# Layer one's last eight modulation groups: ScalarE multiplies and GpSimd adds, and TensorE sums over partitions only

## The chip, the cores and the metric

The kernel runs as one launch on one core of a Trainium2 chip. The core has five engines that the trace names PE (TensorE matrix multiplications; PEld is its weight load), DVE (VectorE), ACT (ScalarE), POOL (GpSimd) and SP (SyncE, which here only issues DMAs), and 16 DMA engines. Each engine works through its own list of instructions in order and waits for the others by semaphores. The metric is the device time of one execution in microseconds, lower is better.

## The reference, cut to what matters

The reference is a two-layer decoder trunk on 1,024 tokens of width 1,024. Per layer a mixer (a gated MLP, a dilated attention with 8 heads, and an S5 state-space part, on slices of one input projection `w_in`, joined by `w_out`) is followed by a grouped mixture of experts. Both are framed by layer norms that are shifted, scaled and gated by a modulation vector, and that vector is what the change is about:

```python
cond = silu(c)                                  # 1,024 numbers
for l in range(DEPTH):                          # two layers
    mod = cond @ ada_w[l] + ada_b[l]            # (1024) x (1024 x 6144): 25 MB of weights a layer
    sh1, sc1, g1, sh2, sc2, g2 = split(mod, 6)  # 1,024 columns each
    h = layer_norm(x) * (1 + sc1) + sh1
    ...                                         # mixer on h -> mix
    x = layer_norm(ALPHA * x + (1 + g1) * mix) * ln1_g[l] + ln1_b[l]
    h2 = layer_norm(x) * (1 + sc2) + sh2
    ...                                         # experts on h2 -> ffn
    x = layer_norm(ALPHA * x + (1 + g2) * ffn) * ln2_g[l] + ln2_b[l]
```

All of it is in float32.

## The kernel before, in words

**Modulation columns.** The 6,144 columns of a layer are worked in 12 groups of 512. A group is eight tiles `ada_w` of 128 partitions x 512 columns (256 KB), since the 1,024 rows lie as 8 rows on each of 128 partitions. Groups 0 to 3 of the first layer (sh1, sc1) are needed before anything else and have a function of their own, `ada_first`. The other eight (groups 4 and 5 are g1, 6 and 7 sh2, 8 and 9 sc2, 10 and 11 g2) are made by `ada` (L924), beside the main work. `ada` starts a second task that loads the eight tiles of each group in order into three buffers of the tag `ada_w`, and then has two forms, chosen by its last argument `pe`:

```python
if pe:                                           # before, for these eight groups
    yield ("until", self.fl.on(w)[1] + late)
    ...
    self.ada_mm(pb, self.csel[:, k], w, k == 0, k == 7)
    self.free(w)
    continue
yield ("until", self.fl.on(w)[1] + 0.5)
t = self.a.activation(w, w, AF.Copy, scale=self.csel[:, k, 0:1])   # ScalarE, in place
if acc is None:
    acc = w
else:
    yield ("until", t)
    self.g.tensor_add(acc, acc, w)                                 # GpSimd
    self.free(w)
...
self.ada_mm(pb, self.ones[:, 0:32], acc, True, True)               # once a group
```

`ada_mm` (L974) is four matrix multiplications of 128 columns, one for each quarter of the tile, on four quarters of the array. So the first form issues 8 x 4 of them a group, the second 4. In the trace each of these float32 multiplications leaves two records: four of them are a row "x8". In both forms `ada_end` (L979) adds the bias on DVE (`ada_m`) and stores the group in the DRAM row `modrow`; `ada_ready` then lets the readers go: the scaling of `w_out` by g1, the rows `sc` and `sh` ahead of the second norm, and the gate of the experts. The second layer's twelve groups already take the second form (calls at L2461 and L2528), six during the first layer's experts and six at the second layer's entry.

**Order of the work.** The kernel is written as tasks (Python generators) with priorities. While it is built, a planner (`Flow`, L115) steps through the tasks by a model of when each engine and each tile comes free, and the order in which instructions are recorded is the order in which every engine executes them. On the chip nothing is reordered. A change of one task's instructions therefore moves the others too.

**The first layer's stages.** Tokens are worked in eight tiles of 128. `project` multiplies each normalised tile (`hT`, split into two fp32r parts, three multiplications a product) with the columns of `w_in`: values and the S5 input, then the gated MLP's `uv`, then keys, then queries; these are the rows `bankA<-wu,hT`. Beside it the task `prep` makes the S5 weights of layer one (`ssm_setup`, `ssm_quarter`: tiles `s_CA`, `s_W`, `s_K`, `s_V`, with DVE and POOL working on them) and stores them as `ssm`. `s_turn` transposes the S5 input (`bankB<-ident,U`), `s5` runs the scan in four quarters (tiles `z`, `t1`, `X`; POOL clears a column of `X`), with the queries' weights let go when its second quarter loads. Attention (`kT`, `qT`, `PT`, `O`) follows, then the output projection (`mix`), then the experts.

Of the kernel before, what the change touches and what calls it, by code (L numbers as in the profile page):

```python
# [327 lines left out]
class Trunk:  # L328
# [2094 lines left out]
    def begin(self, l):  # L2423

        fl, I = self.fl, self.I
        ev = lambda n=NT: [Event() for _ in range(n)]
        self.a_ready, self.b_ready, self.q_ready, self.k_ready = ev(), ev(), ev(), ev()
        self.hT_ready, self.s_ready, self.mix_done, self.chosen = ev(), ev(), ev(), ev(2)
        self.c_ready, self.b_left, self.left, self.late_left = Event(), [4] * NT, [4, 4], 2 * NT
        self.pa_open, self.kq_open, self.at_open, self.s5_go = ev(4)  # L2430
        self.vc, self.vc_ready, self.entered = [None] * 2, ev(2), ev()
        self.hT, self.q = [None] * NT, [None] * NT
        pa_s, kq_s = ExitStack(), ExitStack()
        b = SimpleNamespace(pa_s=pa_s, kq_s=kq_s, prep=None, sb=None)
        if l:
            self.small = NT
            self.front(l)
        ln, bc = self.ln, self.bc
        if l == 0:
            st, sb = ExitStack(), ExitStack()  # L2440
            sets = self.ssm_loads(0, self.pool(sb, "ssm_in", "right"))
            tp = self.pool(st, "prm", "right")
            loads = self.param_loads(tp)
        if l:
            ins = [fl.spawn(self.enter_on(l, i, ln, bc), (0.5 if i < HANDED else 4.4) + i / 100) for i in range(NT)]
        else:
            ins = [fl.spawn(self.enter(l, t, ln, bc), t[0]-2) for t in ((0,), (1,), (2, 3), (4, 5), (6, 7))]
        uv, us, ua = self.w_first
        uk, uq = self.w_in(l, 1024), self.w_in(l, 512)
        if l == 0:  # L2450
            fl.spawn(self.ada_first(), -1)
            for u in uq:
                u.hold = self.s5_go
            for u in uv:
                u.more, u.hold = self.wpools, self.shifted
            self.weights([u for us in self.w_first for u in us] + uk + uq)

            fl.spawn(self.ada([(0, n) for n in range(4, 12)], self.hT_ready[1]), 4)
            b.sb, b.prep = sb, fl.spawn(self.prep(st, tp, loads, sets), 4)
        else:  # L2460
            fl.spawn(self.ada([(1, n) for n in range(6, 12)], self.hT_ready[3], 3.0, False), 4)  # L2461
            for u in uk:
                u.hold = self.s5_go
            self.weights(uk + uq)
        tails, gm, qk, vs = [], [], [], []
        task = lambda to, f, *a: to.append(fl.spawn(f(*a), 3))


        def first():
            yield from self.project([(uv, 512, lambda i, pb: task(vs, self.v_after, l, i, pb)),  # L2470
                                     (us, 256, lambda i, pb: task(tails, self.s_after, l, i, pb, ln))])


        def second():
            yield ("wait", m1)
            yield from self.project([(ua, 512, lambda i, pb: task(gm, self.gmlp, l, i, pb))])

        def keys():
            yield ("wait", m2)
            yield from self.project([(uk, 512, lambda i, pb: task(qk, self.k_after, i, pb))])  # L2480

        def queries():
            yield ("wait", mk)
            yield from self.project([(uq, 512, lambda i, pb: task(qk, self.q_after, i, pb))], True)
        m1 = fl.spawn(first(), 6 if l else 5)
        m2 = fl.spawn(second(), 5)
        mk = fl.spawn(keys(), 5)
        mq = fl.spawn(queries(), 5)

        def left():  # L2490
            yield ("wait", m2)
            for e in gm:
                yield ("wait", e)
            pa_s.close()
            self.pq = self.pool(kq_s, "pq", "left")
            self.kT = self.loose(self.pool(kq_s, "kT", "left").tile([128, 4, T], F32, name="kT"))
            self.kq_open.at = fl.now
        b.ins, b.m1, b.mq, b.left, b.tails, b.qk, b.vs = ins, m1, mq, left, tails, qk, vs
        return b
# [208 lines left out]
```

## Time and profile before

| what | us |
|---|---|
| runs (three) | 2178.49, 2185.55, 6393.65; median 2185.55 |
| the profiled execution, its own time | 2174.52 |
| its span, first to last instruction | 2172.7 |
| PE busy | 1939.7 (89%) |
| DVE busy | 1186.0 (55%) |
| ACT busy | 747.2 (34%) |
| POOL busy | 312.0 (14%) |
| `ada_w` groups on ACT (second form, 12 groups) | 67.3 |
| `ada_w` sums on POOL (second form, 12 groups) | 118.8 |

The profiled execution took 2174.52 us, 1.8 us more than its span; the two runs near it took 4 and 11 us longer. Busy shares are means over the whole span; the change lies between 57 and about 560 us of it. A row of groups reads: line, engine, operation, result <- operands, shapes, count | busy us, mean ns of one | idle us of the engine ahead of them and what ended most of it.

### The profile page before, as it was taken

How to read it: one execution, taken by the hardware profiler on the slowest of the kernel's cores; microseconds unless marked ns; L12 is line 12 of the kernel's file. 1: busy time of each engine (PE TensorE's matmuls, PEld its weight loads, DVE VectorE, ACT ScalarE, POOL GpSimd, SP SyncE). 2: the span in 40 equal slices, each digit the busy share in tenths (PEclk: the TensorE clock that was granted, in tenths of full speed). 3: DMA queues.
4: the chain of work that ended last, by engine and by line, in shares of the span. 5: the costliest groups of instructions: out<-in, count | busy, mean ns of one | idle time of the engine just before them, and what ended most of it. 6: DMA issues, size and time to landing. Idle time of an engine off the chain costs nothing. (4 is left out here: it accounts for less than half of the span.)

```text
span 2172.7 us, 32497 instructions
## 1 busy us (share of the span) xinstructions
PE 1939.7 (89%) x12034; PEld 1341.7 (62%) x12034; DVE 1186.0 (55%) x2891; ACT 747.2 (34%) x1372; POOL 312.0 (14%) x304
## 2 busy tenths in 40 slices
PE   5988999989899999897888989999799999999782
PEld 3866777668653656556557777766685465655640
DVE  7857634556862744435377575455576332443536
ACT  2321145533322424324247334564213131332431
POOL 0024000100113233210002211020000101111000
PEclk9999999999999999998889999999899999999896
DMA  7565632145748899897764544331673769989782
GB/s 267 176 200 167 228 131 79 51 150 179 270 160 293 254 332 341 292 320 234 265 184 161 175 121 126 94 104 59 209 239 126 260 217 309 318 309 306 214 294 100
DMA packets 186822, 451.51 MB, mean 208 GB/s; under 512 B 28968, under 2 KB 80376, under 8 KB 169636
## 3 DMA queue, kind: packets, MB, share of 16 engines
q1 hardware_dynamic: 169584, 393.60, 51.9%
q0 software_dynamic: 15584, 55.24, 10.5%
q8 instruction: 96, 1.57, 0.3%
q10 hardware_dynamic: 1492, 0.56, 0.1%
q14 instruction: 66, 0.54, 0.1%
HBM read 366.66 MB, written 83.01 MB: 207 GB/s over the span
## 5 line engine op out<-in xcount | busy, mean ns | idle before, releaser
L467 PE MATMUL bankA<-wu,hT 128*128 128x512 f32 (+2 forms) x3202 | 834.1, 415 | 27.4 <-DMA hT<-mixT 15.3
L467 PEld LDWEIGHTS bankA<-wu,hT 128*128 128x128 f32 (+1 forms) x3202 | 561.5, 190 | 208.8 <-issue 76.4
L467 PE MATMUL bankA<-hT 128*128 128x512 f32 (+1 forms) x834 | 260.2, 476 | 10.3 <-ACT hT L110 6.7
L110 DVE TENSOR_TENSOR wu<-raw,wu 128x1024 fp32r<-128x1024 f32 x122 | 151.7, 1248 | 161.7 <-ACT wu L110 160.6
L110 ACT ACTIVATE hT<-bankB 128x512 fp32r<-128x512 f32 (+1 forms) x174 | 99.4, 595 | 355.8 <-PE bankB L480 335.7
L467 PE MATMUL bankY<-wu,hT 128*128 128x512 f32 (+1 forms) x584 | 207.1, 520 | 5.0 <-ACT hT L110 4.1
L467 PEld LDWEIGHTS bankA<-hT 128*128 128x128 f32 (+1 forms) x834 | 143.4, 183 | 81.8 <-issue 43.5
L110 ACT ACTIVATE wu<-raw 128x1024 fp32r<-128x1024 f32 x122 | 128.8, 1060 | 157.3 <-DMA raw<-in_exp_w_gate_dram 40.6
L110 POOL TENSOR_TENSOR ada_w<-ada_w 128x512 f32<-128x512 f32 x84 | 118.8, 1415 | 349.8 <-ACT ada_w L110 343.5
L467 PEld LDWEIGHTS bankY<-wu,hT 128*128 128x128 f32 (+1 forms) x584 | 104.0, 188 | 76.3 <-issue 54.9
L110 DVE TENSOR_TENSOR hT<-bankB,hT 128x512 fp32r<-128x512 f32 x114 | 75.4, 686 | 113.8 <-ACT hT L110 113.7
L366 POOL DMA_INDIRECT xa<-g,rc_idx x40 | 68.4, 1709 | 460.2 <-DVE g L110 358.6
L110 DVE TENSOR_TENSOR hT<-raw,hT 128x1024 fp32r<-128x1024 f32 x61 | 75.9, 1249 | 86.0 <-ACT hT L110 85.6
L467 PE MATMUL bankY<-hT 128*128 128x512 f32 (+1 forms) x310 | 104.1, 511 | 8.7 <-ACT hT L110 8.4
L110 DVE SCALAR_TENSOR_TENSOR g<-bankY,rc_wsl,mod 128x512 f32<-128x512 f32 x68 | 48.4, 747 | 81.6 <-PE bankY L467 80.3
L467 PE MATMUL bankC<-wu,hT 128*128 128x512 f32 (+1 forms) x256 | 84.1, 480 | 6.1 <-ACT wu L110 2.1
L110 ACT ACTIVATE hT<-raw 128x1024 fp32r<-128x1024 f32 x61 | 64.4, 1059 | 71.3 <-DMA raw<-in_exp_w_up_dram 24.8
L110 ACT ACTIVATE ada_w<-ada_w,csel 128x512 f32<-128x512 f32 x96 | 67.3, 719 | 60.0 <-DMA ada_w<-in_ada_w_dram 58.4
L467 PEld LDWEIGHTS bankY<-hT 128*128 128x128 f32 (+1 forms) x310 | 53.8, 189 | 46.1 <-issue 24.0
L110 ACT ACTIVATE hT<-hT,mx 128x256 f32<-128x256 f32 (+7 forms) x128 | 70.8, 558 | 2.6 <-DVE mx L110 2.5
L480 PE MATMUL bankB<-ident,hT 128*128 128x128 f32 x384 | 62.4, 289 | 6.5 <-ACT hT L110 2.9
L110 ACT ACTIVATE mhT<-bankB 128x512 f32<-128x512 f32 x32 | 19.2, 599 | 141.7 <-PE bankB L480 141.7
(496 smaller groups left out, 2614.9 us busy)
## 6 DMA issues: line engine op xcount, KB each, us to landing
ada_w<-in_ada_w_dram SPq DMA_DIRECT2D x160, 256.0 KB
raw<-in_exp_w_gate_dram SPq DMA_DIRECT2D x48, 512.0 KB
raw<-in_exp_w_up_dram SPq DMA_DIRECT2D x48, 512.0 KB
raw<-in_exp_w_down_dram SPq DMA_DIRECT2D x48, 512.0 KB
wu<-in_exp_w_down_dram SPq DMA_DIRECT2D x23, 1024.0 KB
hT<-in_exp_w_up_dram SPq DMA_DIRECT2D x20, 1024.0 KB
wu<-in_exp_w_up_dram SPq DMA_DIRECT2D x19, 1024.0 KB
wu<-in_exp_w_gate_dram SPq DMA_DIRECT2D x19, 1024.0 KB
```

The costliest lines, as they stand in the source:

```text
L110: f(*a, **k)
L366: self.nc.gpsimd.indirect_dma_start(out=rows, out_offset=bass.IndirectOffsetOnAxis(ap=ix, axis=0), in_=x, in_offset=None, compute_op=OP.add)
L467: self.nc.tensor.matmul(out, l, r, start=start, stop=stop, **kw)
L480: self.nc.tensor.transpose(out, x, self.ident[:k, :k] if perm is None else perm)
```

## The change

One call is changed: the eight groups 4 to 11 of layer one now take the second form of `ada` instead of the first. Loads, bias, store and the waiting readers stay as they are written.

```diff
-            fl.spawn(self.ada([(0, n) for n in range(4, 12)], self.hT_ready[1]), 4)
+            fl.spawn(self.ada([(0, n) for n in range(4, 12)], self.hT_ready[1], 3.0, False), 4)
```

It removes 256 multiplications of TensorE (512 records) that stood in 48 places of its list, and adds 32 (64 records) in 8 places, 64 multiplications of ScalarE and 56 additions of GpSimd. The DMAs are the same; the planner places them, and much else, anew.

TensorE, in the gated MLP's part of the projection (`uv`, `gt` are the MLP's tiles, `s_CA`, `s_W` the S5 weights). Before:

```order
L467 MATMUL bankA<-wu,hT 128x512 x6
L480 MATMUL bankB<-ident,gt 128x128 x2
L467 MATMUL bankC<-ada_w,csel 32x128 x4
L467 MATMUL bankA<-wu,hT 128x512 x6
L467 MATMUL bankC<-ada_w,csel 32x128 x4
L480 MATMUL bankB<-ident,s_W 128x128 x4
L467 MATMUL bankA<-wu,hT 128x512 x12
L467 MATMUL bankB<-uv,gm_wt 128x64 x4
L467 MATMUL bankC<-ada_w,csel 32x128 x4
```

and now:

```order
L467 MATMUL bankB<-uv,gm_wt 128x64 x4
L467 MATMUL bankA<-wu,hT 128x512 x12
L480 MATMUL bankB<-ident,gt 128x128 x2
L467 MATMUL bankA<-wu,hT 128x512 x6
L480 MATMUL bankB<-ident,s_W 128x128 x4
L467 MATMUL bankA<-wu,hT 128x512 x6
L467 MATMUL bankB<-uv,gm_wt 128x64 x4
```

The small bursts are gone from between the projection's rows. In the whole list 48 bursts (36 of x4, 8 of x8, 4 of x12) have become 8 of x4.

GpSimd, from the last of the S5 weights (`s_W`) through the S5 scan (`X`) to the attention's stores (`mixT`). Before:

```order
L110 TENSOR_TENSOR s_W<-s_W,s_t_2272 128x256
L110 MEMSET zero 128x1024
L110 MEMSET ada_b 128x128
L110 MEMSET X 128x2 x6
L110 MEMSET ada_b 128x128
L110 MEMSET X 128x2 x2
L356 DMA mixT_73<-hT 128x4x128 x16
```

and now:

```order
L110 TENSOR_TENSOR ada_w<-ada_w 128x512 x3
L110 MEMSET X 128x2 x2
L110 TENSOR_TENSOR ada_w<-ada_w 128x512 x2
L110 MEMSET X 128x2 x2
L110 MEMSET ada_b 128x128
L110 TENSOR_TENSOR ada_w<-ada_w 128x512 x2
L110 MEMSET X 128x2 x2
L110 TENSOR_TENSOR ada_w<-ada_w 128x512 x2
L110 MEMSET X 128x2 x2
L110 TENSOR_TENSOR ada_w<-ada_w 128x512 x3
L110 MEMSET ada_b 128x128
L110 TENSOR_TENSOR ada_w<-ada_w 128x512 x7
```

GpSimd had nothing between the S5 weights and the attention's stores but small clears; now 26 of the 56 additions stand ahead of the first clear of `X`, 6 between the clears, and 24 behind the last, down to the attention's end.

SyncE's queue, from the S5 part's last stores (`ss`) to the output projection's first tile (`mx` is the residual). Before:

```order
L356 DMA mixT_73<-ss 128x512 x8
L356 DMA ada_w<-modrow 128x512 x2
L356 DMA raw<-in_w_out_dram 128x2x512 x2
L356 DMA hT<-vd_71 128x2048
L356 DMA raw<-in_w_out_dram 128x2x512
L356 DMA hT<-vd_71 64x2048
L356 DMA raw<-in_w_out_dram 128x2x512
L356 DMA hT<-mixT_73 128x8x128 x2
L356 DMA raw<-in_w_out_dram 128x2x512 x4
L356 DMA hT<-mixT_73 128x8x128 x2
```

and now:

```order
L356 DMA raw<-in_w_out_dram 128x2x512 x2
L356 DMA ada_w<-in_ada_w_dram 128x512 x3
L356 DMA hT<-mixT_73 128x8x128 x2
L356 DMA modrow<-ada_m 4x128
L356 DMA ada_b<-in_ada_b_dram 4x128
L356 DMA ada_w<-in_ada_w_dram 128x512 x8
L356 DMA modrow<-ada_m 4x128
L356 DMA ada_b<-in_ada_b_dram 4x128
L356 DMA ada_w<-in_ada_w_dram 128x512 x4
L356 DMA raw<-in_w_out_dram 128x2x512 x2
L356 DMA ada_w<-in_ada_w_dram 128x512
L356 DMA raw<-in_w_out_dram 128x2x512 x2
```

Before, all loads of `ada_w` for layer one were behind the queue when `w_out` was loaded; now the last two groups' loads stand among those of `w_out`, and they end ahead of the output projection's second tile.

## Rows read from the trace of the kernel before

**Rows 1.** Stages: start:end, length, busy (count) by engine, PE clock, DMA share, GB/s
```profile
57.00:330.00 273.00, 255.86 (x1781) 195.66 (x1780) 172.16 (x524) 72.46 (x128) 36.74 (x67) 0.96 0.56 179
330.00:480.00 150.00, 143.36 (x1960) 103.50 (x1959) 77.88 (x279) 75.65 (x205) 12.30 (x16) 1.00 0.26 78
1200.00:1445.00 245.00, 230.60 (x1615) 179.59 (x1615) 136.12 (x411) 107.07 (x219) 46.82 (x49) 0.98 0.41 127
```

**Rows 2.** Groups of instructions on PE, 57 to 330 us: the first form
```profile
L467 PE MATMUL bankC<-ada_w,csel 128*32 128x128 f32 x512 | 24.6, 288 | 2.2 <-DMA ada_w<-in_ada_w_dram 2.2
```

**Rows 3.** Timeline of PE, 62 to 230 us: start, length, instruction, count
```profile
62.03 0.86 PE L467 MATMUL bankC<-ada_w,csel 128*32 128x128 f32 x24
62.83 0.63 PE L467 MATMUL bankA<-wu,hT 128*128 128x256 f32 x3
...
161.01 1.66 PE L467 MATMUL bankA<-wu,hT 128*128 128x512 f32 x6
162.60 0.43 PE L467 MATMUL bankC<-ada_w,csel 128*32 128x128 f32 x8
166.56 1.94 PE L467 MATMUL bankB<-uv,gm_wt 128*128 128x64 f32 x8 [3.54 <-DVE uv L110]
...
221.24 8.50 PE L467 MATMUL bankA<-wu,hT 128*128 128x512 f32 x36
229.58 1.00 PE L467 MATMUL bankB<-uv,gm_wt 128*128 128x64 f32 x8
```

**Rows 4.** Timeline of PE, 1215 us: the second form's sum over partitions
```profile
1215.06 0.43 PE L467 MATMUL bankC<-ada_w,ones 128*32 128x128 f32 x8
1215.42 3.02 PE L467 MATMUL bankA<-wu,hT 128*128 128x512 f32 x12
```

**Rows 5.** The page's groups: the second form's other instructions, 12 groups
```profile
L110 POOL TENSOR_TENSOR ada_w<-ada_w 128x512 f32<-128x512 f32 x84 | 118.8, 1415 | 349.8 <-ACT ada_w L110 343.5
L110 ACT ACTIVATE ada_w<-ada_w,csel 128x512 f32<-128x512 f32 x96 | 67.3, 719 | 60.0 <-DMA ada_w<-in_ada_w_dram 58.4
```

**Rows 6.** Timeline of POOL, then DVE, then PE, 1284 to 1289 us
```profile
1284.44 2.75 POOL L110 TENSOR_TENSOR ada_w<-ada_w 128x512 f32<-128x512 f32 x2 [2.12 <-ACT ada_w L110]
...
1284.65 1.43 DVE L110 TENSOR_TENSOR X<-z,wu 128x254 f32<-128x254 f32 x1
1286.00 1.48 DVE L110 TENSOR_TENSOR t<-z,wu 128x254 f32<-128x254 f32 x1
...
1287.85 0.41 DVE L110 TENSOR_TENSOR X<-z,wu 128x254 f32<-128x254 f32 x1
...
1288.08 0.49 PE L467 MATMUL bankY<-wu,X 64*128 64x128 f32 x4 [2.91 <-DVE X L110]
```

**Rows 7.** Stages as in rows 1, behind the two waits for DVE
```profile
166.00:172.00 6.00, 5.44 (x24) 4.18 (x24) 2.40 (x4) 0.36 (x2) 0.14 (x1) 0.50 0.51 154
1289.00:1296.00 7.00, 6.80 (x28) 5.47 (x29) 3.85 (x7) 0.66 (x2) 0.00 (x0) 0.52 0.64 208
```

**Rows 8.** Timeline of DVE: one step of a short chain, at two places
```profile
161.94 1.35 DVE L110 SCALAR_TENSOR_TENSOR rs_y<-rs_t,rs_g 128x1 f32<-128x1 f32 x1
...
1225.42 0.16 DVE L110 SCALAR_TENSOR_TENSOR rs_y<-rs_t,rs_g 128x1 f32<-128x1 f32 x1
```

**Rows 9.** Waits of SP's queue, 57 to 290 us, then 1200 to 1445 us: total, times, longest
```profile
SPq L356 <- PE bankC L467: 60.3, 26, 5.8
...
SPq L356 <- POOL ada_w L110: 74.8, 19, 9.2
```

**Rows 10.** Timeline of POOL: the attention's stores, layer one, then layer two
```profile
366.34 1.81 POOL L356 DMA_DIRECT2D mixT<-hT  x2 [100.29 <-ACT PT L110]
...
429.79 1.50 POOL L356 DMA_DIRECT2D mixT<-hT  x2 [9.42 <-ACT hT L110]
...
1413.59 1.69 POOL L356 DMA_DIRECT2D mixT<-hT  x2
...
1476.73 1.50 POOL L356 DMA_DIRECT2D mixT<-hT  x2 [9.42 <-ACT hT L110]
```

## The prediction

> **What bounds the kernel now.** The page gives PE 89% of the span and no other engine over 55%, but the change lies in a piece of it, so I read the stages first. From 57 to 330 us (projection, S5 weights, S5 scan) PE is busy 255.86 of 273 us and DVE 172.16; in the attention, 330 to 480 us, PE is busy 143.36 of 150 us [rows 1]. PE sets the pace in both: 17.1 us of idle in the first, 6.6 in the second. The groups of PE's instructions then give what the change takes away: 512 records of the first form, 24.6 us busy [rows 2]. They are interleaved with the projection, so what a burst costs must be read from the timeline, from its start to the next instruction's start [rows 3]. Last I looked for the second form elsewhere in the same trace, since layer two already runs on it: its entry, 1200 to 1445 us, has the same projection, S5 scan and the attention's start, with PE busy 230.60 of 245 us [rows 1], and its ACT and POOL instructions stand in the page's groups [rows 5]. The chain of waits is no help here: it ends a few microseconds before the end of the span.
>
> **PE, removed.** 48 bursts: 36 of 4 multiplications, 8 of 8, 4 of 12. A burst of 12 (24 records) takes 0.80 us from its start to the next row's, 62.03 to 62.83 [rows 3]; one of 4 (8 records) 0.36, 1215.06 to 1215.42 [rows 4]; 8 lie midway, 0.58. That is 36 x 0.36 + 8 x 0.58 + 4 x 0.80 = 20.8 us. A burst also breaks the projection's stream: 6 multiplications ahead of a burst take 1.59 us (161.01 to 162.60), while 36 in one go take 8.34 (221.24 to 229.58), 1.39 for 6 [rows 3]. So a break costs 0.2 us; in the order before, 17 bursts lie between two rows of the projection: 3.4 us. **Added:** 8 bursts of 4, 8 x 0.36 = 2.9 us [rows 4]. Net 21.3 us less work on the engine that sets the pace. The bounds are 17.9 (no break is saved) and 27.5 (all 48 are).
>
> **ACT, added.** 64 multiplications of 0.719 us, 46 us [rows 5], beside 72.46 us of work in 273 and 75.65 in 150 [rows 1]: the engine is far from full. But it works in order, and it stood idle 60.0 us ahead of 96 such multiplications, 58.4 of them for the tile's DMA [rows 5]. That is 0.63 us each, 40 us for 64, during which evictions of PE's banks queue behind. Their cover is the three banks of the projection.
>
> **POOL, added.** 56 additions of 1.415 us, 79 us [rows 5], where POOL is busy 36.74 of 273 and 12.30 of 150 [rows 1]. It has the time; behind it queue the products of the S5 weights, the clears of `X` and the attention's 16 stores. The last I cost at nothing: from the first store to the one at 429.79 layer one's attention took 63.45 us, and from 1413.59 to 1476.73, with layer two's last additions and multiplications in between, 63.14 [rows 10].
>
> **DVE, slowed.** This is the price to find. When POOL made two additions at 1284.44 us, two products of DVE took 1.43 and 1.48 us, where the same one takes 0.41 two rows on; PE waited 2.91 us for `X` [rows 6]. Behind that, its clock was granted at 0.52 for 7 us, between the levels of 1.2 and 2.4 GHz and near the lower, against 1.00 ahead: another 7 x 0.48 = 3.4 us [rows 7]. The first layer knows this already, from POOL's S5 products: a one-column step took 1.35 us instead of 0.16 [rows 8], PE waited 3.54 us for `uv` [rows 3], and the clock stood at 0.50 for 6 us [rows 7]. So an addition can hold DVE for nothing up to 1.07 us (1.48 less 0.41), and a held DVE can cost PE twice.
>
> The Trainium skill, "SBUF — State Buffer", section "Who interferes with whom", says that a DVE instruction with two inputs in SBUF and a GpSimd instruction that reads SBUF exclude each other for the whole instruction, and that whichever starts first blocks the other. The trace agrees: 1.43 and 1.48 us against 0.41 [rows 6]. By that rule alone every addition would be a loss of its whole length to DVE, and the sum below would turn; it is the second rival.
>
> **The new waits together** (ACT's and DVE's). From below nothing. From above, all of PE's idle time in layer two's entry, 245 less 230.60, 14.4 us [rows 1], and 3.4 of half clock: 18. That stage has about as many additions as the first layer will have up to its attention (26 ahead of the clears of `X`, 6 between them). I take one event like that at 1284 us, 2.91 + 3.4 = 6.3 us, and 4 us for evictions behind ACT's waits and shorter stretches: 10 us. It is nearer to the middle than to nothing, because DVE's steps in the first layer are many and small.
>
> **SP and the readers, moved.** The same 64 loads wait for buffers that POOL frees instead of PE. Before, the queue stood 60.3 us for PE's bursts in 233 us; in layer two's entry it stands 74.8 for POOL's additions in 245 [rows 9]. Behind it wait the weights of `w_in` and, new, half of `w_out`'s. I cost that at nothing: the second half of `w_out` is needed only behind the attention, and the readers of g1 need groups 4 and 5, which stay the first. If a load falls late there, the queue's 9.2 us is the longest wait [rows 9].
>
> **Sum.** 2174.5 - 21.3 + 10 = 2163.2 us against the profiled execution. That one is the fastest shown: two of the three runs took 4.0 and 11.0 us more (the third, 6393.65, is left out), and the mean of the three near ones is 5 us above it. So the forecast for a median is **2168 us**. After the attention nothing absorbs the lead: no instruction is tied to a clock, so loads and stages start as much earlier.
>
> **Rivals.**
> *More of it arrives (0.13).* The lead of 27.5 us at most with no new wait: 2174.5 - 27.5 + 5 = 2152. For it: ACT and POOL have room, and layer two's entry idles no larger a share of its stage than layer one's (14.4 of 245, 17.1 of 273) [rows 1]. Against it: that entry has a wait of 2.91 us that the additions made [rows 6].
>
> *The additions hold DVE on the path (0.12), slower than before.* 32 additions up to the end of the clears of `X`, each holding DVE for 1.04 us, the mean of the two stretches [rows 6], 33 us; all of it on the path against 21.3 saved gives +12: 2174.5 + 12 + 5 = 2191. It decides from 20 held steps that PE waits for (21.3 / 1.04), or from four events with half clock (21.3 / 6.3). Against it: DVE is busy 63% of the stage [rows 1], so many additions meet it idle or in an instruction on a bank.
>
> *No gain (0.25).* PE's work is less, but the S5 weights and the gated MLP's chain on DVE end as late as before, and PE waits there for what it saved. DVE's 172 us with 32 halves of 1.04 is 189 in a stage that would last 252, 75%, and in the S5 weights it is denser. 2174 to 2184, about 2179. Against it: PE has queued keys to work on while DVE builds the S5 weights.
>
> *The forecast* keeps 0.50. The changed call does move the work, as the order shows, so that it does nothing is no case.
>
> **Numbers.** The range is 2150 to 2192: below it lie the best part of the first rival, above it the end of the second, or the third with a median like the upper of the two runs. Faster or slower by 2% means 43 us, about what a measurement of this kernel can tell from no change: more than the whole of the removed bursts, and more than all held steps less the saving. The chances left for both come from the order that the planner lays anew behind the change: faster 0.03, within 2% 0.93, slower 0.04.
>
> **What would show it.** Right: no first-form rows, 64 records of the second form on PE; PE's idle time up to the attention 20 to 30 us; the attention's first store 5 to 18 us before 366; DVE's one-column steps of over 0.5 us beside additions; POOL's additions near 1.4 us. Wrong: the first store at or behind 366 us; half clock in more than two stretches of 6 us; ACT's waits for `ada_w` that PE inherits for more than 5 us; a wait of the output projection for `w_out` or `modrow`.

## The result, and the profile after

The changed kernel took **2195.82 us** (median of four runs, 2192.84 to 2205.44) against 2182.02 of the kernel before on the same chip: a ratio of **1.0085, 95% interval 1.0058 to 1.0113**, so it is slower, though within the 2% to which the prediction gave 0.93. The ratio leaves out one run of 6393.65 us, which stands in that median; the three others of the kernel before took 2175.43, 2178.49 and 2185.55 us. A second set of runs of the same two kernels gave 1.0072 (1.0050 to 1.0094). The forecast was 2168, with a range of 2150 to 2192: wrong in sign and outside the range. The profiled execution of after took 2193.53 us, with a span of 2191.7.

The page's line of engines, and behind it the stages of [rows 1] (the columns are the same):

```profile
PE 1922.3 (88%) x11586; PEld 1337.9 (61%) x11586; DVE 1211.8 (55%) x2890; ACT 784.1 (36%) x1437; POOL 395.0 (18%) x360
...
57.00:330.00 273.00, 233.07 (x1305) 186.02 (x1304) 186.59 (x510) 94.97 (x165) 92.15 (x103) 0.93 0.47 146
330.00:480.00 150.00, 141.05 (x1911) 100.24 (x1909) 84.26 (x282) 91.32 (x231) 34.84 (x34) 0.95 0.39 115
```

The work moved as planned: up to 330 us PE is busy 22.8 us less, ACT 22.5 and POOL 55.4 more. But PE's idle time there went from 17.1 to 39.9 us, and DVE, which got nothing to do, is busy 14.4 us more. The groups of instructions that answer to [rows 2] and [rows 5]:

```profile
L467 PE MATMUL bankC<-ada_w,ones 128*32 128x128 f32 x64 | 3.4, 284 | 0.2 <-DVE O L110 0.2
...
L110 POOL TENSOR_TENSOR ada_w<-ada_w 128x512 f32<-128x512 f32 x140 | 198.6, 1418 | 609.5 <-ACT ada_w L110 591.4 <-issue 8.9 <-DMA raw<-in_w_in_dram 7.2
L110 ACT ACTIVATE ada_w<-ada_w,csel 128x512 f32<-128x512 f32 x160 | 112.5, 716 | 90.9 <-DMA ada_w<-in_ada_w_dram 80.8 <-POOL mk_J L110 10.0
```

No row of the first form is left, and there are 56 more additions and 64 more multiplications at the lengths that [rows 5] gave. What DVE's extra time is shows in its timeline, in the chain of small steps that builds the S5 tables; the rows answer to [rows 6, 8]. POOL first, then DVE:

```profile
110.32 2.69 POOL L110 TENSOR_TENSOR ada_w<-ada_w 128x512 f32<-128x512 f32 x2 [0.56 <-ACT ada_w L110]
...
110.09 0.17 DVE L110 TENSOR_TENSOR turn<-turn,sc_cos 128x16 f32<-128x16 f32 x1
110.18 0.17 DVE L110 TENSOR_TENSOR t<-turn,sc_sin 128x16 f32<-128x16 f32 x1
110.38 1.27 DVE L110 TENSOR_TENSOR turn<-turn,t 128x16 f32<-128x16 f32 x1
111.57 0.16 DVE L110 TENSOR_TENSOR turn<-turn,sc_sin 128x16 f32<-128x16 f32 x1
111.69 0.17 DVE L110 TENSOR_TENSOR t<-turn,sc_cos 128x16 f32<-128x16 f32 x1
111.90 1.15 DVE L110 TENSOR_TENSOR turn<-turn,t 128x16 f32<-128x16 f32 x1
```

Two steps of 0.17 us that start while an addition runs end with it: they take 1.27 and 1.15 us. For every DVE instruction that overlaps an addition I took its length less the lower quartile of its own kind, and call the sum held time: up to 330 us it is **20.9 us in 26 steps**, for 38 additions. In before no addition ran there.

PE's clock next, in stages of 6 us as in [rows 7], and what PE waited for from 57 to 330 us (total, times, longest):

```profile
136.00:142.00 6.00, 1.09 (x4) 0.72 (x4) 0.00 (x0) 0.00 (x0) 0.00 (x0) 0.50 0.96 350
142.00:148.00 6.00, 2.42 (x5) 1.62 (x6) 3.65 (x6) 3.50 (x5) 2.16 (x2) 0.50 0.23 50
148.00:154.00 6.00, 3.23 (x9) 2.02 (x8) 5.90 (x10) 2.00 (x2) 2.86 (x2) 0.50 0.70 195
...
190.00:196.00 6.00, 6.00 (x30) 4.25 (x29) 3.58 (x13) 0.00 (x0) 0.00 (x0) 0.50 0.46 154
```

```profile
PE bankA L467 <- ACT wu L110: 7.8, 1, 7.8
PE bankB L480 <- DVE gt L110: 6.1, 4, 3.5
PE bankB L480 <- DVE q L110: 5.6, 1, 5.6
PE bankB L467 <- DVE at L110: 5.1, 1, 5.1
PE bankB L480 <- DMA gm_lg<-in_gm_ln_g_dram: 4.0, 1, 4.0
PE bankA L467 <- DVE wu L110: 3.6, 3, 2.8
```

From 136 to 154 us PE works 6.7 of 18 us, at 0.50, which is the level of 1.2 GHz; it had idled for 3.8 of the 6 us ahead. One stretch at 0.50 follows at 190, where PE is busy throughout, behind 6 us in which it worked 0.86. ACT and DVE stand still in the stretch from 136 to 142: ACT's longest waits (57 to 350 us) and SP's for POOL (57 to 290 us, answering to [rows 9]) tell why.

```profile
ACT s_C L110 <- DMA rc_rw<-in_router_w_dram: 14.1, 1, 14.1
ACT ada_w L110 <- POOL mk_J L110: 10.0, 1, 10.0
...
SPq L356 <- POOL ada_w L110: 49.6, 17, 11.7
```

ACT and DVE both go on with the S5 preparation when the router's weights (`rc_rw`) have landed, and that load stands in SP's queue. It was issued at 140.6 us instead of 129.7. DVE's chain ahead was 7.5 us late. Besides, in the new order four loads for the gated MLP (`uv` and three more) stand ahead of the eight stores of zeros and of this load; before, they stood behind them. SP's queue, the changed kernel first, then before:

```profile
133.40 0.38 SPq L356 DMA_DIRECT2D uv<-in_gm_ws_dram  x1
...
135.45 5.10 SPq L356 DMA_DIRECT2D ssm<-zero  x8
140.59 0.70 SPq L356 DMA_DIRECT2D rc_rw<-in_router_w_dram  x1
```

```profile
125.17 4.44 SPq L356 DMA_DIRECT2D ssm<-zero  x8
129.66 0.65 SPq L356 DMA_DIRECT2D rc_rw<-in_router_w_dram  x1
...
138.96 0.38 SPq L356 DMA_DIRECT2D uv<-in_gm_ws_dram  x1
```

The attention's first store, which answers to the first row of [rows 10], comes 8.2 us later than before:

```profile
374.55 1.81 POOL L356 DMA_DIRECT2D mixT<-hT  x2
...
441.51 1.52 POOL L356 DMA_DIRECT2D mixT<-hT  x2 [2.62 <-ACT hT L110]
```

From the first of these stores to the sixth pair the attention took 67.0 us, where [rows 10] gave 63.45. The first expert's load was issued at 566.7 us, before at 555.9.

### The profile page after: what moved, and what is told of

Same layout as the page of the kernel before. It is cut to its first block, busy times and chain, and to the rows that moved or that the text cites. A ratio compares the mean times of both kernels' runs of the same rounds, so it can differ in the third digit from the quotient of the medians.

```text
span 2191.7 us, 31770 instructions
## 1 busy us (share of the span) xinstructions
PE 1922.3 (88%) x11586; PEld 1337.9 (61%) x11586; DVE 1211.8 (55%) x2890; ACT 784.1 (36%) x1437; POOL 395.0 (18%) x360
## 5 line engine op out<-in xcount | busy, mean ns | idle before, releaser
L467 PE MATMUL bankA<-wu,hT 128*128 128x512 f32 (+2 forms) x3250 | 854.6, 417 | 37.4 <-DMA hT<-mixT 11.8
L467 PEld LDWEIGHTS bankA<-wu,hT 128*128 128x128 f32 (+1 forms) x3250 | 577.1, 192 | 211.6 <-issue 68.0
L110 POOL TENSOR_TENSOR ada_w<-ada_w 128x512 f32<-128x512 f32 x140 | 198.6, 1418 | 609.5 <-ACT ada_w L110 591.4
L467 PE MATMUL bankA<-hT 128*128 128x512 f32 (+1 forms) x754 | 238.0, 473 | 5.1 <-DVE hT L110 2.4
L110 ACT ACTIVATE hT<-bankB 128x512 fp32r<-128x512 f32 (+1 forms) x174 | 99.1, 594 | 338.8 <-PE bankB L480 317.7
L467 PEld LDWEIGHTS bankA<-hT 128*128 128x128 f32 (+1 forms) x754 | 131.1, 182 | 74.6 <-issue 46.4
L110 ACT ACTIVATE ada_w<-ada_w,csel 128x512 f32<-128x512 f32 x160 | 112.5, 716 | 90.9 <-DMA ada_w<-in_ada_w_dram 80.8
L467 PE MATMUL bankY<-hT 128*128 128x512 f32 (+1 forms) x354 | 117.0, 503 | 11.1 <-ACT hT L110 9.0
L467 PEld LDWEIGHTS bankY<-hT 128*128 128x128 f32 (+1 forms) x354 | 61.0, 186 | 45.6 <-issue 19.7
L467 PE MATMUL bankC<-wu,hT 128*128 128x512 f32 (+1 forms) x242 | 76.8, 473 | 1.8 <-ACT wu L110 1.1
L467 PE MATMUL bankC<-hT 128*128 128x512 f32 (+1 forms) x222 | 73.9, 521 | 0.8 <-DVE hT L110 0.8
```

Source lines behind the costliest of these rows:

```text
L110: f(*a, **k)
L467: self.nc.tensor.matmul(out, l, r, start=start, stop=stop, **kw)
```

## The experiments

Three theories stood at the start. **Held DVE**: the additions read SBUF, hold DVE's steps in the S5 preparation, and PE ends up waiting. **Queues**: the tiles' way through SP, ACT and POOL blocks what stands behind them in these in-order queues. The third, **order**, says that the planner's new order is worse whatever the additions take.

Some runs leave out part of the sums. The router then sends other tokens to the experts, so their totals cannot be compared with the rest (they came out at 1.0544 for c, 1.1828 for e, 1.0030 for a and 1.0647 for b). The expectations of these four were written in totals, so they decide little as they stand. All runs are read at two marks ahead of the experts: the attention's first store, and the first expert's load, both counted from the first transposition of `x` (the DMAs ahead of it differ by some 5 us between executions). Profiled executions of the same kernel differ by up to 2.5 us at the first mark and 3.5 at the second (run m has before's instructions up to there, so it is a third execution of it; the means below are of the first two). Most runs below have one profiled execution, so differences of that size say nothing. Runs h, q and the two mixed ones have an order that the planner laid anew, and m has one behind the second mark; the others keep the order of before or of the changed kernel up to that mark.

| run | first store | first expert's load | total against before (95%) |
|---|---|---|---|
| before; again | 325.6; 325.0 | 515.1; 511.6 | 1 |
| changed; again | 333.1; 331.1 | 525.3; 523.1 | 1.0085 (1.0058 to 1.0113); 1.0072 (1.0050 to 1.0094) |
| c: before, short bursts | 318.4 | 503.8 | not comparable |
| e: changed, additions and multiplications short | 319.8 | 510.0 | not comparable |
| a: changed, additions short | 322.0 | 515.0 | not comparable |
| b: changed, fills for additions; again | 322.4; 323.1 | 517.9; 515.7 | not comparable |
| s: changed, fills in four groups | 325.9 | 518.8 | not comparable |
| p: changed, additions in four pieces | 336.6 | 533.0 | 1.0109 (1.0080 to 1.0138) |
| f: before and 40 additions | 332.2 | 521.2 | 1.0053 (1.0035 to 1.0071) |
| g: before and 40 multiplications | 332.9 | 521.3 | 1.0060 (1.0039 to 1.0080) |
| h: four groups moved to the attention | 322.9 | 522.1 | 1.0052 (1.0036 to 1.0068) |
| k: changed, zero stores on ACT | 332.9 | 528.4 | 1.0077 (1.0052 to 1.0102) |
| k: before, zero stores on ACT | 324.6 | 513.7 | 1.0002 (0.9979 to 1.0025) |
| q: product and sum on DVE | 317.5 | 519.0 | 1.0014 (0.9991 to 1.0037) |
| four groups on DVE, four on PE | 327.5 | 531.7 | 1.0101 (1.0070 to 1.0131) |
| five groups on DVE, three on PE | 317.6 | 517.2 | 1.0045 (1.0025 to 1.0066) |
| m: layer two's first six groups on PE | 323.1 | 511.6 | 1.0033 (1.0009 to 1.0057) |

**One part at a time, in the changed kernel's own order.** The planner is told of the full instruction and the engine gets a short one, so that nothing else moves.

```diff
-  self.g.tensor_add(acc, acc, w)
+  a: tensor_add(acc[:, 0:16], acc[:, 0:16], w[:, 0:16])      # first layer only
+  b: memset(w, 0.0), three times                             # as long, but reads nothing
+  e: as a, and activation(w[:, 0:16], w[:, 0:16], ...) for ScalarE's
```

> Left out: in layer one's last eight groups GpSimd adds 16 of a tile's 512 columns, so 56 additions of 1.4 us become about 0.2 us; the order of every engine is that of the changed kernel. Held-DVE theory (the additions hold DVE's instructions in the S5 preparation, that chain ends late, PE waits): most of the loss goes, 2168 to 2182 us against 2196 of the changed kernel. Queue theory (the tiles' way through SP, ACT and POOL blocks what is queued behind them; DVE only follows): tiles come free 1.2 us earlier, 2188 to 2194. Order theory (the planner's new order is worse by itself, whatever the additions take): 2193 to 2199.

> Left out: each of those 56 additions is replaced by three fills of its 128x512 tile on GpSimd, together about 1.4 us (one fill of this size took 0.53 us in the trace of before): POOL is as long busy, but reads nothing. Held-DVE theory, in the form that it is the reading of two inputs that holds DVE: DVE's stretched steps go and the time falls as with short additions, 2168 to 2182 us. Queue theory and order theory: tiles come free as late as in the changed kernel, 2192 to 2200.

> Left out: additions and ScalarE's multiplications of those eight groups on 16 of 512 columns; order as in the changed kernel. Held-DVE theory: as the run with short additions alone, within 3 us. Queue theory: ACT gets 64 x 0.5 us back and tiles come free 0.5 us earlier: 4 to 10 us below the run with short additions alone. Order theory: 2190 to 2199, close to the changed kernel.

The stage of 57 to 330 us, first of the run with fills, then of the run with both short:

```profile
57.00:330.00 273.00, 240.01 (x1360) 191.68 (x1358) 167.13 (x546) 102.42 (x183) 103.61 (x188) 0.94 0.50 157
```

```profile
57.00:330.00 273.00, 240.15 (x1362) 192.60 (x1360) 168.86 (x544) 84.51 (x182) 52.38 (x106) 0.94 0.50 157
```

With fills POOL is busier than with additions (103.61 against 92.15), yet DVE is back at 167.13 from 186.59, its held time is 0.3 us instead of 20.9, and the first store comes at 322.4 and 323.1 instead of 333.1 and 331.1. So **9.3 us of the loss up to the first store are the additions' reading**; their time on POOL alone is 0.8 (b less a), and ACT's multiplications 2.2 (a less e), both no larger than what two executions differ by. The price of the reading is what the held-DVE theory says. The queue theory gave 4 to 10 us for the multiplications; at the second mark they are 5.0, so it is not ruled out there. Two steps take 2.20 and 2.30 us in the changed kernel at 86 to 89 us, beside two additions; in the second execution of b the same two take 1.28 us each beside six fills. The rows are first of the changed kernel, then of b:

```profile
85.28 4.54 POOL L110 TENSOR_TENSOR ada_w<-ada_w 128x512 f32<-128x512 f32 x2 [3.79 <-ACT ada_w L110]
...
86.48 2.20 DVE L110 SCALAR_TENSOR_TENSOR x<-x,rs_y,sh 128x1024 f32<-128x1024 f32 x1
88.61 2.30 DVE L110 SCALAR_TENSOR_TENSOR x<-x,bn_m,sc 128x1024 f32<-128x1024 f32 x1
```

```profile
86.24 3.54 POOL L961 MEMSET ada_w<- 128x512 f32 x6 [3.39 <-ACT ada_w L110]
...
87.52 1.28 DVE L110 SCALAR_TENSOR_TENSOR x<-x,rs_y,sh 128x1024 f32<-128x1024 f32 x1
88.72 1.28 DVE L110 SCALAR_TENSOR_TENSOR x<-x,bn_m,sc 128x1024 f32<-128x1024 f32 x1
```

The Trainium skill, "SBUF — State Buffer", section "Who interferes with whom", has a DVE instruction with two inputs in SBUF contend with a GpSimd instruction that reads SBUF and not with one that only writes it; these rows agree, 2.20 beside additions and 1.28 beside fills.

> The run with fills once more: first store within 2 us of 360.8, first expert's load within 3 us of 556.3. Anything above 367 would unsettle the price put on the additions' reading.

It came at 365.5 and 558.1 us, uncorrected: 4.7 above the first execution at the first mark, more than expected, but below the 367 that would have unsettled the price. Its first transposition was 4.0 us later too; counted from there the two executions are 0.7 us apart.

**The saving on PE alone, in the order of before.**

```diff
-  self.ada_mm(pb, self.csel[:, k], w, k == 0, k == 7)         # 4 x 32x128
+  self.ada_mm(...) if k == 0 else matmul(pb[0:32, 128:144], csel[:, k], w[:, 0:16])
```

> The kernel before, in its own order, with the change's saving on PE alone: seven of the eight bursts of a group are one multiplication of 16 columns (left out: seven eighths of the sum of those eight groups), 56 x (0.36 less about 0.1) = 12 to 15 us less on PE. If PE's work sets the end of the stage, as the prediction has it: 2167 to 2172 us against 2182. If PE waits in the S5 stage for DVE's chain anyway (no gain): 2178 to 2184.

From a burst's start to the next row's, the 48 bursts take 21.8 us in before and 11.1 here (the short ones still take 193 ns a record), so 10.7 us left PE. The first store comes 6.9 us earlier than before's mean, the first expert's load 9.6. The saving is real, and in the old order most of it arrives: 6.9 of 10.7 us by the attention, 9.6 by the first expert's load. PE hardly waits longer there: from the first transposition to the first store it idles 26.6 us, in before 25.0 and 24.6.

Run e has 19.0 us off PE (2.8 us of bursts left), short operations on ACT and POOL, and the new order. PE is busy 276.8 us up to the first store, in before 300.5 and 300.4. But it idles 43.0 us there, and only 5.5 us arrive at the first mark and 3.4 at the second. So **of the 23.6 us that PE is busy less, some 18 became waiting, although the operations that the change adds to ACT and POOL are short here**. Part of the order theory holds: in the new order most of the saving is lost. Run e also takes 8.3 us more off PE than run c; that this alone, in the old order, would have uncovered new waits was not tested. What PE waits for in e is the S5 preparation; run e, total, times, longest:

```profile
PE bankA L467 <- ACT wu L110: 8.3, 1, 8.3
PE bankB L480 <- DMA wu<-ssm: 7.6, 1, 7.6
PE bankB L467 <- DVE at L110: 5.6, 1, 5.6
```

The first of these waits ends when ACT goes on behind the router's weights. Counted from the first transposition, that load is issued at 88.9 and 90.5 us in before, 84.6 in c, 95.8 in e, and 99.1 and 99.3 in the changed kernel. So some 6 us of its delay stay when both operations are short, and the additions' reading adds about 3 (95.4 in a, 96.6 and 95.8 in b). How much of the first store hangs on this load was not isolated.

**One part added to before.** In place on a tile that has just landed, so that values stay: five of eight tiles a group.

```diff
+  f: tensor_add(w, w, zeros[:, 0:1].to_broadcast([128, 512]))  # GpSimd
+  g: activation(w, w, AF.Copy, scale=ones[:, 0:1])             # ScalarE
```

> The kernel before, in its own order and with its bursts on PE, plus 40 additions on GpSimd (five of each of the eight groups): a tile just loaded plus a column of zeros, in place, so the values stay. The additions come without ACT's multiplications and without the accumulator's buffer. Held-DVE theory: 40 additions of about 1.4 us, each holding DVE up to 1.2 us when they meet, with about half of that on the path: 6 to 15 us slower than before. Queue theory: the additions alone do little, 0 to 4 us slower. If DVE's chain has slack: no difference, -2 to +2.

> The kernel before, in its own order and with its bursts, plus 40 multiplications by one on ScalarE (five of each of the eight groups), in place on the tile just loaded, in ACT's queue at the place where the planner sees the tile landed. Queue theory: ACT stands for tiles that are late and holds evictions back: 5 to 12 us slower than before. Held-DVE theory: 0 to 4 us slower.

Both cost about 7 us at the first store (332.2 and 332.9 against 325.3) and 0.5 to 0.6% in all. But neither measures its part cleanly, because the burst now has to wait for the instruction in front of it. PE's first wait in f, then in g:

```profile
PE bankC L467 <- POOL ada_w L949: 12.0, 4, 6.4
```

```profile
PE bankC L467 <- ACT ada_w L949: 9.4, 8, 2.8
```

In f DVE's held time is 16.9 us (its additions, with a single column as second operand, take 1.04 us in the median); how the 7 us divide between that and PE's 12.0 us of waiting for POOL stays open. g comes out just above the queue theory's range (13 us), f within the held-DVE theory's (12 us), both partly by a wait that the changed kernel doesn't have. The prices above are taken from the runs a, b and e.

**Where, and for how long.**

```diff
+  s: fills for groups 4 to 7, additions for groups 8 to 11
+  p: for q in range(4): tensor_add(acc[:, c], acc[:, c], w[:, c])   # c: 128 columns
```

> Left out: the additions of groups 4 to 7, with three fills each in their place (POOL as long busy, nothing read); groups 8 to 11 are added as in the changed kernel; its order. Only the time up to the first expert's load is comparable, since the experts get other tokens. If the loss is made in the S5 preparation (up to 220 us): first store at 361 to 364 us, close to the 360.8 of the run with all fills. If it is made in the scan and the attention's start: 370 to 374.

> The changed kernel in its own order, each of the 56 additions cut into four of 128 columns; the sums are the same. If an addition holds DVE to its end, and a DVE instruction gets in between two pieces, a held step loses at most some 0.4 us instead of up to 1.2: DVE's stretched time ahead of 330 us falls from 21 us to 6 to 12, the attention's first store comes at 366 to 371 us instead of 374.7, and the total is 4 to 9 us below the changed kernel. If GpSimd keeps what holds DVE from one piece to the next: first store 374 to 378, total the same or up to 4 us longer.

Neither of the two outcomes of s came: with 325.9 it lies between the fills (322.8) and the additions (332.1). So, by this one execution, 6.2 us of the reading's price are made by groups 4 to 7 and 3.1 by groups 8 to 11. My hope for p fell altogether. The pieces and two of DVE's steps beside them:

```profile
L962 POOL TENSOR_TENSOR ada_w<-ada_w 128x128 f32<-128x128 f32 x224 | 114.6, 545 | 251.9 <-ACT ada_w L110 247.1 <-issue 4.6
```

```profile
108.02 3.53 POOL L962 TENSOR_TENSOR ada_w<-ada_w 128x128 f32<-128x128 f32 x8
...
109.11 0.33 DVE L110 TENSOR_TENSOR turn<-turn,t 128x16 f32<-128x16 f32 x1
...
109.91 0.39 DVE L110 TENSOR_TENSOR turn<-turn,t 128x16 f32<-128x16 f32 x1
```

A held step now loses 0.2 us instead of 1.0 to 1.1, as expected: DVE gets in between two pieces. But the additions take 114.6 us instead of 78.0, and 69 steps are held instead of 26: 15.9 us in sum instead of 20.9, and the tiles come free later. The first store comes 4.5 us later than in the changed kernel although DVE is held less; which of the two costs does that was not separated. With 1.0109 it has the highest ratio of all, not clear of the changed kernel's own.

**The same work on DVE.**

```diff
+  q: self.v.scalar_tensor_tensor(acc, w, self.csel[:, k, 0:1], acc, op0=OP.mult, op1=OP.add)
+  mixed: the same for n < 8 (or n < 9), PE's bursts from there on
```

> The changed kernel with product and sum of tiles two to eight of each of the eight groups in one instruction on DVE (56 of some 0.7 us, 39 us), in an order that the planner lays anew; ACT multiplies only the first tile, GpSimd adds none of them. DVE's added 39 us stand against 21 us of held steps ahead of the attention and 56 x 0.7 = 39 us less on ACT. If held time is the price: first store 368 to 374, 0 to 8 us below the changed kernel. If DVE's load in the S5 preparation is the price: first store 375 to 385, 0 to 12 us above it.

> Groups 4 to 7 with product and sum of tiles two to eight on DVE, groups 8 to 11 by PE's bursts as before; nothing on GpSimd. The groups end at about the attention's start. First store 360 to 364 us (before: 364.4 to 366.3), and the attention and the mixing behind it as long as before, 188 us: the first expert's load 2 to 5 us ahead of before's, total 2 to 5 us below it. If DVE's 22 us in the S5 preparation are on the path: first store 366 to 370.

> The same with five groups on DVE and three by PE's bursts: first store 358 to 363 us; the last group ends inside the attention, which gives 0 to 4 us back: total 0 to 6 us below before.

```profile
L110 DVE SCALAR_TENSOR_TENSOR ada_w<-ada_w,csel 128x512 f32<-128x512 f32 x56 | 43.1, 769 | 3.8 <-DMA ada_w<-in_ada_w_dram 3.1 <-ACT ada_w L110 0.5
```

DVE does product and sum itself for 43.1 us, and the first store comes at 317.5, 14.6 us ahead of the changed kernel; in all q is level with before. Ahead of the first store lie 32 of the 56 instructions, 25.2 us. So ScalarE's multiplications and GpSimd's additions together, the latter without an instruction on DVE, cost this stage more than 25 us of DVE's own work. The planner's order is new in q, so this is no clean price. Behind the first store q takes 201.5 us to the first expert's load (before 188.1), which gives back more than it had gained. The two mixed versions were to keep the gain and did not: four groups 1.0101, five 1.0045. With four even the first store is late, 327.5. PE's longest wait is the same in all three, 12 us for `gm_lg`, a load in SP's queue, so it does not tell them apart. What does is PE's work ahead of the store: 285.9 us busy and 41.6 idle with four groups, 276.9 and 40.7 with five. The planner put 12 bursts and some of the attention's multiplications ahead of the store in the former, so there the first mark is not the same point of the work. No version beat before.

**Other places and orders.**

```diff
+  h: ada(groups 4 to 7, hT_ready[1]); ada(groups 8 to 11, at_open, 3.0, False)
+  k: the eight stores `ssm<-zero` on ACT's queue instead of SP's
+  m: before, with ada(layer two's groups 0 to 5, mixed) in the first form
```

> Groups 4 to 7 by PE's bursts as before; groups 8 to 11 by ScalarE and GpSimd, and begun when the attention begins. PE loses 28 of the 64 tile bursts, 28 x 0.36 = 10 us. In the attention DVE does little that PE waits for, and no step of the S5 preparation meets an addition. Held-DVE theory and queue theory alike: 3 to 9 us faster than before. Order theory: anywhere from 8 us faster to 8 us slower.

h came out slower, 1.0052, where its expectation had 3 to 9 us faster. It has its first store 2.4 us ahead of before's mean, and loses 11.1 from there to the first expert's load (199.2 against 188.1); PE idles 15.7 us there, in before 8.3 and 6.6. So the attention does not take the four groups for nothing; whether their loads, their multiplications, their additions or the new order cost it was not separated. The stage of 330 to 480 us:

```profile
330.00:480.00 150.00, 135.51 (x1922) 96.09 (x1921) 74.38 (x254) 87.27 (x221) 41.15 (x41) 0.96 0.36 105
```

> The changed kernel in its own order, with eight stores moved: the zeros into the S5 buffers go out on ACT's queue, which stood idle there, instead of SP's, where they were issued 5.1 us long behind six loads. All values stay. If what is left between the run with short bursts and the run with both operations short (about 6 us at the first expert's load) comes from the place of these stores, by which DVE and ACT stand until the router's weights have landed: DVE and ACT go on 4 to 6 us earlier, PE's wait of 7.8 us for ACT shrinks, and the first expert's load comes at 560 to 563 us; total 4 to 7 us below the changed kernel. If that wait only uncovers DVE's held chain behind it: 565 to 567, total within 2 us.

> The same eight stores moved in the kernel before, in its own order. PE's own wait at this place is 2.0 us there: 0 to 3 us faster, the first expert's load at 553 to 556.

The edit did not do what it was for. In the changed kernel the eight stores took 11.59 us to issue on ACT (5.10 on SP), and DVE and ACT then stood for these stores instead of the router's weights: counted from the first transposition DVE went on at 102.7 us, without the edit at 102.2 and 102.5. The first expert's load, at 571.4 us, came later than both outcomes had it. In before the stores took 5.03 us on ACT (4.44 on SP), and nothing changed either. Whether the place of these stores makes the difference between runs c and e (1.4 us at the first mark, 6.2 at the second) stays open.

```profile
130.80 11.59 ACTq L2360 DMA_DIRECT2D ssm<-zero  x8
```

> The kernel before, with layer two's first six groups, which are summed by ScalarE and GpSimd during layer one's experts, given to PE's bursts: 42 bursts of 0.36 us more on PE, 15 us, in a stage where the queues move weights at 0.9 of their time; 42 additions fewer, which hold DVE for some 10 to 17 us there. If held DVE is worth more than PE's bursts in this stage too: 2 to 10 us faster than before. If PE's time sets it: 5 to 12 us slower. Either is possible; about even.

Slower, 1.0033 (1.0009 to 1.0057), though in an order laid anew: as it stands, the second form is the better one during layer one's experts, although its additions hold DVE there by 16.6 us in before. The trade that loses in the S5 stage does not lose there.

> The changed kernel once more, unchanged, on the chip of the other runs of this call: 8 to 20 us slower than before; its profile shows how far the stages differ from one profiled execution to the next (I expect the first expert's load within 4 us of 566.7).

> The kernel before once more, unchanged, for a second profiled execution: the first expert's load within 2 us of 555.8; the end up to 10 us later than 2172.7, since the first profile was among the shortest executions.

The changed kernel's first expert's load came at 566.9 us, in its first profile at 566.7; before's at 551.1 and 555.9, further apart than I expected. Before's end was 3.2 us later than in the first profile.

## Why the prediction was wrong

**PE, removed: the size was right, its way into the sum was the step that failed.** 19.0 us of bursts left PE, and up to the first store it was busy 23.6 us less (run e); the prediction had 17.9 without breaks and 21.3 with those it counted. But it booked them whole, as "less work on the engine that sets the pace", because PE was busy 255.86 of 273 us [rows 1]. With the change's operations on ACT and POOL short and in the new order 5.5 us of them reach the first store (run e), in the old order 6.9 of 10.7 (run c). So in the old order most of what was booked would have come; what the new order costs was put at nothing. In the new order PE runs through the projection's rows sooner and then stands for the S5 preparation, which is DVE's chain with SP's loads and ACT's evictions. PE's idle time up to the first store is 25.0 and 24.6 us in before, 26.6 in c, 43.0 in e, and 48.5 and 49.5 in the changed kernel; the prediction's own sign of being right was 20 to 30. That is the third rival's mechanism ("no gain"), which was set aside because PE has queued keys to work on; the order that decides it was named only among the chances left for 2%.

**The new waits: mis-sized, less so.** The term was 10 us. Up to the first store ACT's multiplications cost 2.2, POOL's time 0.8 and the additions' reading 9.3: 12.3 us. The split was wrong: one event of 6.3 us was booked for DVE, but 26 steps were held. That is above the second rival's point of 20, though PE does not wait for each of them. That rival had the mechanism and the sign; its price was too high (33 us of held time, 20.9 measured; all of it on the path, 9.3 measured), and its saving too (21.3).

**The sum at the first store:** before 325.3; 5.5 arrives, 12.3 is added, 332.1. The prediction had 21.3 and 10. Of the 18 us between the two, 15.8 are the saving that did not arrive, 2.3 the waits. Step by step, from means of the profiled executions of each run, at both marks:

| step | first store | first expert's load |
|---|---|---|
| shorter bursts, order of before (c less before) | -6.9 | -9.6 |
| new order, 8.3 us more off PE, short operations on ACT and POOL (e less c) | +1.4 | +6.2 |
| ACT's multiplications in full (a less e) | +2.2 | +5.0 |
| POOL as long busy, nothing read (b less a) | +0.8 | +1.8 |
| the additions' reading (changed less b) | +9.3 | +7.4 |
| sum (changed less before) | +6.8 | +10.8 |

With executions of one kernel that differ by up to 2.5 and 3.5 us, the reading and the saving in the old order stand clear of that, and so does the new order at the second mark; the other steps do not.

**POOL and the attention at nothing: off by about 4 us, the cause not shown.** From the first store to the first expert's load it takes 192.1 us instead of 188.1 (189.5 and 186.7). The additions are not what costs it: with them short it takes 193.1 us (run a), with the multiplications short too 190.3 (run e). What is left is of the size by which two executions differ.

**SP at nothing: wrong in kind.** The readers of g1 and the output projection waited for nothing new, as said. SP's longest wait for POOL was 11.7 us, where the prediction had 9.2 at most, but it lies at 245 us, behind the S5 preparation. What came late was the load of the router's weights, by its new place in SP's queue and by DVE's chain ahead. What this alone costs was not isolated.

**What would show it.** Of its signs of being right the records of the second form, the additions' length and DVE's held one-column steps came (`rs_y` took 1.08 us at 169.15 beside an addition, 0.16 without), PE's idle time and the first store did not. First store at 374.55, half clock in four stretches of 6 us, ACT's wait handed on to PE for 7.8 us: each was named as a sign of error. Six of the projection's multiplications took 2.91 us at 0.50 (at 191.40) and 1.64 behind it (at 200.02). By that ratio the four stretches cost PE some 6 us at most (about half of its 12.7 us busy), an estimate; it is part of the prices above and does not come on top.

**Behind the first expert's load** the changed kernel took 1625.0 and 1635.8 us, before 1616.8 and 1624.8. The loss up to there is 10.8 us counted from the first transposition; by the ratios the totals differ by 16 to 19. The rest lies where two executions of one kernel differ by 8 to 11 us, and is left open.

## What to carry to other kernels

An engine that is busy 94% of a stage sets its end only as long as what it waits for keeps up. Before booking a saving on it, ask which chain its last wait in the stage belongs to, and shorten the work twice: once without moving the order, to see how much arrives, and once in the new order with the added operations short, to see what the order costs. Here the first gave 6.9 of 10.7 us, the second 5.5 of 19.0. An instruction handed to GpSimd that reads SBUF is paid by DVE where DVE's chain of two-input steps is what others wait for, here with 9.3 us; hand over such work where DVE's results are not waited for, and compare with letting DVE do it. Cutting the instruction into pieces shortens each hold and multiplies the holds.

## What the runs showed of the hardware that was not expected

- Fills of GpSimd hold DVE for next to nothing (0.3 us in 123 fills up to 330 us), additions of less total length for 20.9. A step with one operand in a bank was not held beside an addition: `t<-bankY,wu` took 0.41 us at 264.70, and `z<-z,t` behind it, with both in SBUF, 1.08.
- An addition of 128x512 takes 1.29 us (median), one of 128x128 0.46: four pieces take 1.4 times as long as the whole.
- Eight stores of 128x512 zeros took 11.59 us to issue on ACT's queue where they took 5.10 on SP's (changed kernel), and 5.03 where they took 4.44 (before). Why the first is so long stays open.
